# Feature-major products with hi and lo activations in one stream, two PSUM sums, and SBUF in hi/lo pairs

## The chip, the cores and the metric

One core of a Trainium2 chip runs the whole program. Its engines are TensorE (PE, with PEld for the load of a stationary operand), VectorE (DVE), ScalarE (ACT), GpSimd (POOL, not used here after the start) and SyncE (SP, which issues most transfers). The metric is the device time of one execution in microseconds (us); lower is better.

## The reference

Two layers of a hybrid block over 256 tokens of width 1024, all in float32. Everything that matters here is a product of activations with a weight matrix:

```python
for l in range(DEPTH):                       # DEPTH = 2
    h = rms_norm(x, norm_mix_pre[l])
    zq, zk, zv, zx, zy, zxq, zg = in_projection(h, w_in[l])
    ...                                      # rotary on q and k
    y_attn = diff_attention(q, k, v, lam, diff_subln[l], lam_init)
    xc = causal_conv(zx, conv_w[l], conv_b[l])
    y_lru = rg_lru(xc, ...) * jax.nn.gelu(zy)
    y_mem = memory_attention(zxq, mem, norm_mem[l], w_kv_mem[l])
    gates = jax.nn.sigmoid(zg.reshape(B, S, N_BRANCH, D_MODEL) + b_gate[l])
    merged = (gates[:, :, 0] * (y_attn @ w_proj_attn[l])
              + gates[:, :, 1] * (y_lru @ w_proj_lru[l])
              + gates[:, :, 2] * (y_mem @ w_proj_mem[l]))
    x = x + rms_norm(merged @ w_out[l], norm_mix_post[l])
    h = rms_norm(x, norm_mlp_pre[l])
    a = jax.nn.relu(h @ w_mlp_up[l])
    x = x + rms_norm((a * a) @ w_mlp_down[l], norm_mlp_post[l])
```

## The kernel before

Each float32 operand of a large product is held as two parts in the rounded type float32r: hi is the value rounded for TensorE, lo is the rest of it. A product is three matmuls: hi·hi, lo·hi and hi·lo.

**Weight stream.** The weights come in chunks of 1 MB, 128 partitions by 2048 values, in the order of their use (`layer_plan`, `full_plan`; 186 chunks: 184 of the two kinds below and twice the gate weights `rg`). SP loads a chunk into one of three `raw` buffers. Each half of a chunk is split by one ACT cast (`wh`, L155) and one DVE subtraction (`wl`, L157), into one of five `hl` buffers each; `weights` runs the splits up to `AHEAD` = 5 halves ahead of their use.

**Feature-major products** (`mm_feat`, L213 to L223) have the weights stationary and the activations moving: a chunk gives two tiles of 128 features by 256 tokens. For each of the two halves and each of eight contraction tiles k there are three matmuls of 256 columns, L219 (wh with the hi part), L220 (wh with the lo part) and L221 (wl with the hi part), all into the same 256 columns of one PSUM tile `acc` (one bank of 512 values, four buffers). They are used for the memory keys (`mk`), the queries of the cross attention (`xq`), the inputs `x` and `y` of the recurrent branch, `q` and `k`, the gates `g0` to `g2`, the branch projections `pm`, `pl`, `pa`, and the `up` product of the MLP: 64 chunks in a layer, 128 in all. **Token-major products** (`mm_tok`, L225 to L252: `mv`, `v`, `wo`, `dn`, 28 chunks in a layer) have the activations stationary and the weights moving, 512 columns in each matmul, three matmuls again (L233, L234, L235).

**Who reads a feature-major sum.** The reader of each chunk takes it straight from PSUM: DVE first in `rotary` (L607 to L610, for q and k), in the `up` product (L877), in the projections (L830, L832) and the memory keys; ACT first for `xq` (a split), `conv` (L530), `gelu2` (L538) and the gates (`tanh`, L822).

**Side work.** The cross attention (`xattn`), the recurrent gates and scan (`lru`), the attention (`attn`) and the transposes (`transposed`) are generators that advance by one step after half chunks (`tick`) or are run to their end (`flush`). Their TensorE work stands between half chunks of the weight stream, in the PSUM pools `at` and `sc`; their DVE and ACT work shares those engines with the splits and with the readers of the sums. A scheduler sets the final order of each engine's queue from the priorities and the dependences; each engine then runs its queue in order.

**SBUF.** Activations take whole buffers of 128 x 2048 values (`a8`, twelve of them), the hi and the lo part each one.

Of the kernel before, what the change touches and what calls it, by code (L numbers as in the profile page):

```python
# [17 lines left out]
D = 1024  # L18
# [7 lines left out]
# vectors of the feature-major parameter tile, 8 columns each  # L26
# [6 lines left out]
def layer_plan(l):  # L33
    """Weight chunks of a layer in the order in which they are used: (name, index)."""
# [34 lines left out]
def trunk(ctx, tc, x_in, xt_in, mem_in, memt_in, w_in, par_in, lamv_in, post_in, rope_in, out):  # L69
# [13 lines left out]
    def a8(name, dt=F32):  # L83
        return p_a8.tile([128, 2048], dt, tag="a8", name=name)
# [13 lines left out]
    def acc():  # L98
        return ps_acc.tile([128, 512], F32, tag="acc", name="acc")
# [4 lines left out]
    # ---------------- constants and parameters  # L104
# [26 lines left out]
    # ---------------- weight stream  # L131
# [14 lines left out]
    def issue_split(u):  # L146
# [6 lines left out]
        lo = p_hl.tile([128, 1024], F32R, tag="wl", name="wl")  # L153
        for sl in ((slice(0, 512), slice(512, 1024)) if u == 0 else (slice(0, 1024),)):
            act.copy(h[:, sl], r[:, sl])  # L155
            with tc.issue_after(state["hold"]) if state["hold"] is not None else nullcontext():
                dve.tensor_tensor(lo[:, sl], r[:, sl], h[:, sl].bitcast(F32), op=ALU.subtract)  # L157
        hl_t[u] = (h, lo)
# [91 lines left out]

    def rsqrt(ss, n, mul):
        """1 / sqrt(ss * mul + eps) of n columns, by Newton steps."""  # L252
# [12 lines left out]
    def rsqrt2(v):  # L265
        """1 / sqrt(v) of each column, the table's value refined by a Newton step."""
# [9 lines left out]
    def transposed(src, gain, h, lo):  # L276
        """Rows of src transposed and times gain, as hi and lo parts."""
        for j in range(4):
# [5 lines left out]
            for i in range(2):  # L284
                f = 2 * j + i
                split_to(f8(h)[:, f, :], f8(lo)[:, f, :], ps[:, i * 256:(i + 1) * 256], gain[:, f:f + 1])
            yield

    def rms(src, junk):
        """1 / rms of the rows of src."""  # L290
# [7 lines left out]
    def normed(src):  # L298
        """RMS-normalised rows of src."""
# [6 lines left out]
    def row_of(r, row):  # L306
        """row[p, token] = r[token] for every p."""
# [48 lines left out]
    # ---------------- parameters worked out once  # L356
# [42 lines left out]
    # ---------------- memory keys and values  # L399
# [4 lines left out]
    def mem_rms():  # L404
        t = a8("memr").rearrange("p (t n) -> p t n", t=2)
        load_rows(t, mem_in)
        j = a8("mj").rearrange("p (t n) -> p t n", t=2)
        dve.tensor_copy(mr, rms(t, j))

    def gained(src, gain, name):  # L410
        """Feature-major rows times gain, as hi and lo parts."""
        h, lo = a8(name + "h", F32R), a8(name + "l", F32R)
        for f in range(8):
            split_to(f8(h)[:, f, :], f8(lo)[:, f, :], f8(src)[:, f, :], gain[:, f:f + 1])
        return h, lo
# [4 lines left out]
    def mem_keys(l, hook=None):  # L420
        kh, kl = a8("kh", F32R), a8("kl", F32R)
        pend = []
        for j in range(4):
            ps = acc()
            mm_feat(ps, (l, "mk", j), mhat[l])
# [3 lines left out]
            if j > 0:  # L429
                for i, p in pend:  # L430
# [3 lines left out]
                    split_to(kh[:, sl], kl[:, sl], k)  # L434
                pend = []
            tick()
        kmem[l] = (kh, kl)

    def mem_values(l, hook=None):
        vh, vl = (a8(n, F32R) for n in ("vh", "vl"))  # L440
        mh, ml = mhat.pop(l)
        for n in range(2):
            pss = [acc(), acc()]
            for c in range(2):
                mm_tok(pss, (l, "mv", 2 * n + c), lambda k: (f8(mh)[:, 4 * c + k, :], f8(ml)[:, 4 * c + k, :]), c == 0, c == 1)
# [4 lines left out]
            for t in range(2):  # L450
                sl = slice(t * 1024 + n * 512, t * 1024 + (n + 1) * 512)
                split_to(vh[:, sl], vl[:, sl], pss[t], mr[:, t:t + 1])
            tick()
        vmem[l] = (vh, vl)

    # ---------------- cross attention (side work)
    def xattn(l, xq, ym):
        qh, ql = (f8(t) for t in xq)
        kh, kl = (f8(t) for t in kmem.pop(l))
# [533 lines left out]
```

## Time and profile before

| | us |
|---|---|
| median of 3 runs (1153.3 to 1154.36) | 1153.54 |
| span of the profiled execution | 1151.0 |
| median less span | 2.5 |
| PE busy, share of the span | 98% |
| DVE busy | 69% |
| ACT busy | 56% |

The span runs from the first to the last instruction of the profiled execution; the times are those of whole executions, so about 2.5 us lie around the span. The profiled execution's own time is not listed apart from the three; its span is the figure that stage by stage sums are made against, and 2.5 us are added to compare with the median. Shares of busy time of PE count a matmul from its start to its modelled end, so that a row's mean is longer than the beat at which matmuls follow each other; the beat is read from the starts in the timeline.

### The profile page before, as it was taken

To read this page: it belongs to the slowest core of one execution; us is meant where nothing else is said; L and a number is where in the kernel's file an instruction comes from. 1 tells how busy PE (TensorE), PEld (TensorE's weight loads), DVE (VectorE), ACT (ScalarE), POOL (GpSimd) and SP (SyncE) were. 2 spreads that over 40 slices of the span, in tenths; PEclk is the share of its full clock that TensorE was granted. 3 is DMA by queue.
4 is the path that set the end of the run, shared out by engine and by line. 5 is a ranking of instruction groups with operands and counts; after the bars stand their busy time and mean duration, and the time that the engine had idled before them with its cause. 6 is when DMAs were issued, how large, how long until landed. Compare 5 with 4: busy or idle time off the path is not lost.

```text
span 1151.0 us, 19712 instructions
## 1 busy us (share of the span) xinstructions
PE 1133.0 (98%) x8144; PEld 1067.1 (93%) x8144; DVE 792.0 (69%) x1219; ACT 644.7 (56%) x984; POOL 0.7 (0%) x6
## 2 busy tenths in 40 slices
PE   7999999999999999999999999999999998999997
PEld 6899999899999899998888999989999997999886
DVE  6868779788756676664557677887876566766453
ACT  6745585665455656554446556846654455655342
POOL 0000000000000000000000000000000000000000
PEclk9999999999999999999999999999999999999999
DMA  9665346643455545555555633664435553555550
GB/s 326 244 220 184 110 167 203 243 156 128 168 213 202 190 169 176 184 171 217 179 210 180 218 111 140 206 226 161 147 147 184 202 183 126 177 184 202 207 185 37
DMA packets 34793, 209.53 MB, mean 182 GB/s; under 512 B 3856, under 2 KB 8080, under 8 KB 10768
## 3 DMA queue, kind: packets, MB, share of 16 engines
q1 hardware_dynamic: 34128, 206.18, 50.2%
q10 hardware_dynamic: 576, 2.10, 0.5%
q8 instruction: 64, 1.05, 0.4%
q14 instruction: 25, 0.20, 0.0%
HBM read 203.02 MB, written 1.05 MB: 177 GB/s over the span
## 4 chain that ended last, share of the span: by engine, by line
PE 97%; DVE 2%; DMA 0%; ACT 0%; issue 0%; SPq 0%; DVEq 0%
PE acc L221 21%; PE acc L219 21%; PE acc L220 21%; PE acc L235 9%; PE acc L234 9%; PE acc L233 9%; PE at L555 1%; PE sc L638 1%; PE at L508 1%; PE at L473 1%; PE at L673 1%; DMA raw<-in_w 0%; PE at L283 0%; DVE wl L157 0%; PE at L493 0%; PE at L688 0%
## 5 line engine op out<-in xcount | busy, mean ns | idle before, releaser
L157 DVE TENSOR_TENSOR wl<-raw,wh 128x1024 fp32r<-128x1024 f32 (+1 forms) x369 | 449.2, 1221 | 258.7 <-ACT wh L155 257.6
L155 ACT CAST wh<-raw 128x1024 fp32r<-128x1024 f32 (+1 forms) x369 | 384.6, 1046 | 384.7 <-PE acc L220 251.4
L219 PE MATMUL acc<-hh,wh 128*128 128x256 f32 x1536 | 438.1, 286 | 0.2 <-ACT hh L209 0.2
L220 PE MATMUL acc<-hl,wh 128*128 128x256 f32 x1536 | 435.0, 283 | 0.5 <-DVE hl L210 0.5
L221 PE MATMUL acc<-hh,wl 128*128 128x256 f32 x1536 | 435.2, 284 | 0.0
L219 PEld LDWEIGHTS acc<-hh,wh 128*128 128x128 f32 x1536 | 294.6, 192 | 1.6 <-ACT wh L155 0.7
L220 PEld LDWEIGHTS acc<-hl,wh 128*128 128x128 f32 x1536 | 295.0, 192 | 1.0 <-DVE hl L210 0.7
L221 PEld LDWEIGHTS acc<-hh,wl 128*128 128x128 f32 x1536 | 294.7, 192 | 0.7 <-issue 0.7
L233 PE MATMUL acc<-wh,sqh 128*128 128x512 f32 x256 | 99.6, 389 | 0.0
L234 PE MATMUL acc<-wl,sqh 128*128 128x512 f32 x256 | 99.6, 389 | 0.0
L235 PE MATMUL acc<-wh,sql 128*128 128x512 f32 x256 | 99.6, 389 | 0.0
L233 PEld LDWEIGHTS acc<-wh,sqh 128*128 128x128 f32 x256 | 48.1, 188 | 10.0
L234 PEld LDWEIGHTS acc<-wl,sqh 128*128 128x128 f32 x256 | 48.1, 188 | 10.0
L235 PEld LDWEIGHTS acc<-wh,sql 128*128 128x128 f32 x256 | 48.1, 188 | 9.8
L219 PE MATMUL acc<-mhh,wh 128*128 128x256 f32 x128 | 38.0, 297 | 6.7 <-ACT wh L155 6.7
L221 PE MATMUL acc<-mhh,wl 128*128 128x256 f32 x128 | 37.5, 293 | 0.7 <-DVE wl L157 0.7
L220 PE MATMUL acc<-mhl,wh 128*128 128x256 f32 x128 | 37.6, 294 | 0.1
L219 PE MATMUL acc<-xqh,wh 128*128 128x256 f32 x128 | 36.8, 288 | 0.0
L219 PE MATMUL acc<-ylh,wh 128*128 128x256 f32 x128 | 36.7, 287 | 0.0
L648 ACT ACTIVATE ae<-sc,anm 128x128 f32<-128x128 f32 (+1 forms) x64 | 26.3, 416 | 18.4 <-DVE anm L644 15.4
L221 PE MATMUL acc<-xqh,wl 128*128 128x256 f32 x128 | 36.4, 285 | 0.0
L221 PE MATMUL acc<-ylh,wl 128*128 128x256 f32 x128 | 36.2, 283 | 0.0
(215 smaller groups left out, 1693.2 us busy)
## 6 DMA issues: line engine op xcount, KB each, us to landing
raw<-in_w SPq DMA_DIRECT2D x183, 1024.0 KB, 4.8
rgw<-in_w SPq DMA_DIRECT2D x2, 1024.0 KB, 6.9
qT<-rq SPq DMA_DIRECT2D x16, 128.0 KB, 2.3
kT<-rk SPq DMA_DIRECT2D x16, 128.0 KB, 2.3
gb<-in_post ACTq DMA_DIRECT2D x4, 512.0 KB, 5.0
mem<-in_memt SPq DMA_DIRECT2D x4, 256.0 KB, 5.7
memr<-in_mem SPq DMA_DIRECT2D x2, 512.0 KB, 7.3
xt<-in_x SPq DMA_DIRECT2D x2, 512.0 KB, 9.5
```

The costliest lines, as they stand in the source:

```text
L155: act.copy(h[:, sl], r[:, sl])
L157: dve.tensor_tensor(lo[:, sl], r[:, sl], h[:, sl].bitcast(F32), op=ALU.subtract)
L219: pe.matmul(o, wh[:, k, :], ah[:, k, :], start=(k == 0), stop=False)
L220: pe.matmul(o, wh[:, k, :], al[:, k, :], start=False, stop=False)
L221: state["mm"] = pe.matmul(o, wl[:, k, :], ah[:, k, :], start=False, stop=(k == 7))
L233: pe.matmul(pss[t], ah[:, sl], wh[:, k, :], start=(first and half == 0 and k == 0), stop=False)
L234: pe.matmul(pss[t], ah[:, sl], wl[:, k, :], start=False, stop=False)
L235: m = pe.matmul(pss[t], al[:, sl], wh[:, k, :], start=False, stop=(last and half == 1 and k == 1))
L473: pe.matmul(o, a[:, k, ts], b[:, k, :], start=(n == 0), stop=(n == 5))
L508: pe.matmul(o, a[:, m, fs], b[:, ms], start=(n == 0), stop=(n == 5))
L555: pe.matmul(ps[:, i * 256:(i + 1) * 256], wv[:, c, f, :], xv[:, f, :], start=True, stop=True)
L648: act.activation(out=e[:, c * nk:(c + 1) * nk], in_=sv[:, c, :], func=AF.Exp, bias=nm[:, c:c + 1], accum_out=ss[:, c:c + 1])
```

## The change

In a feature-major product the hi and the lo part of the activations now stand in one buffer (`pair`, 128 x 4096 values, hi in the first half and lo in the second), and pass wh in one matmul of 512 columns made of two runs of 256: hi·wh lands in columns 0 to 255 of a PSUM bank and lo·wh in columns 256 to 511. wl with the hi part follows as a matmul of 256 columns into columns 0 to 255. Each half of a chunk now fills one bank, so `acc` has two banks and there are two such buffers in place of four of one bank. After the chunk, ACT copies the right halves of both banks to SBUF (`z`, a `tmp` buffer) and DVE adds the left halves; `mm_feat` gives `z` to the reader, which no longer reads PSUM. SBUF is dealt out in six pairs in place of twelve singles; what needs only a single buffer takes a pair (`a8`), or two such needs share one (`duo`). `mm_tok` keeps its matmuls. Comments and docstrings went as well.

```diff
-    p_a8 = ctx.enter_context(tc.tile_pool(name="a8", bufs=12))
+    p_pair = ctx.enter_context(tc.tile_pool(name="pair", bufs=6))
...
-    ps_acc = ctx.enter_context(tc.tile_pool(name="psacc", bufs=4, space=bass.MemoryType.PSUM))
+    ps_acc = ctx.enter_context(tc.tile_pool(name="psacc", bufs=2, space=bass.MemoryType.PSUM))
...
-    def a8(name, dt=F32):
-        return p_a8.tile([128, 2048], dt, tag="a8", name=name)
+    def pair(name):
+
+        return p_pair.tile([128, 4096], F32R, tag="pair", name=name)
...
+    def hl(t):
+
+        return t.rearrange("p (s k n) -> p s k n", s=2, k=8)
+
+    def duo(name):
+
+        t = p_pair.tile([128, 4096], F32, tag="pair", name=name)
+        return t[:, 0:2048], t[:, 2048:4096]
+
+    def a8(name):
+        return duo(name)[0]
...
     def acc():
-        return ps_acc.tile([128, 512], F32, tag="acc", name="acc")
+
+        return ps_acc.tile([128, 2, 512], F32, tag="acc", name="acc")
+
+    def acc_tok():
+        a = acc()
+        return [a[:, t, :] for t in range(2)]
...
-    def mm_feat(ps, key, a):
-        """Two feature tiles of 256 tokens: weights stationary."""
-        ah, al = (f8(t) for t in a)
+    def mm_feat(key, a):
+
+
+
+
+        ps = acc()
+        av = hl(a)
         for j in range(2):
             wh, wl = (f8(t) for t in weights(*key, j))
-            o = ps[:, j * 256:(j + 1) * 256]
+            o = ps[:, j, :]
             for k in range(8):
-                pe.matmul(o, wh[:, k, :], ah[:, k, :], start=(k == 0), stop=False)
-                pe.matmul(o, wh[:, k, :], al[:, k, :], start=False, stop=False)
-                state["mm"] = pe.matmul(o, wl[:, k, :], ah[:, k, :], start=False, stop=(k == 7))
+                pe.matmul(o.rearrange("p (s n) -> p s n", s=2), wh[:, k, :], av[:, :, k, :], start=(k == 0), stop=False)
+                state["mm"] = pe.matmul(o[:, 0:256], wl[:, k, :], av[:, 0, k, :], start=False, stop=(k == 7))
             if j == 0:
                 tick()
+        z = tmp("z")
+        act.copy(two(z), ps[:, :, 256:512])
+        dve.tensor_tensor(two(z), two(z), ps[:, :, 0:256], op=ALU.add)
+        return z
...
-                ps = acc()
-                mm_feat(ps, (l, nm, j), hx)
+                ps = mm_feat((l, nm, j), hx)
                 rotary(scale, j, ps, r)
...
-            pss = [acc(), acc()]
+            pss = acc_tok()
```

**What stands where.** DVE, in the q and k products of the first layer, before: the subtraction for the weights (`wl`), the rotary steps that read `acc`, and a step of the recurrent branch (`xc<-xc,lE`).

```order
L157 TENSOR_TENSOR wl<-raw,wh 128x1024
L607 SCALAR_TENSOR_TENSOR rp_1956<-acc,rope 128x512
L608 SCALAR_TENSOR_TENSOR rp_1957<-acc,rope 128x256
L609 SCALAR_TENSOR_TENSOR rp_1957<-acc,rope 128x256
L157 TENSOR_TENSOR wl<-raw,wh 128x1024
L610 TENSOR_TENSOR rq<-rp_1956,rp_1957 128x2x256
L583 SCALAR_TENSOR_TENSOR xc<-xc,lE 128x512
```

DVE, at the same place, now (`xcg` is the former `xc`, `rqk` the former `rq`):

```order
L253 TENSOR_TENSOR z<-z,acc 128x512
L181 TENSOR_TENSOR wl<-raw,wh 128x1024
L641 SCALAR_TENSOR_TENSOR rp_1682<-z,rope 128x512
L642 SCALAR_TENSOR_TENSOR rp_1683<-z,rope 128x256
L643 SCALAR_TENSOR_TENSOR rp_1683<-z,rope 128x256
L181 TENSOR_TENSOR wl<-raw,wh 128x1024
L644 TENSOR_TENSOR rqk<-rp_1682,rp_1683 128x2x256
L617 SCALAR_TENSOR_TENSOR xcg<-xcg,lE 128x512
```

Each chunk has one more DVE instruction, L253, which stands ahead of a `wl` and waits for the ACT copy L252; the rest kept its order.

ACT, in the y product of the first layer, before: the first reader of the sum (`gq<-acc`) is on ACT, followed by the tanh of the recurrent gate, the second half of the GeLU, and a cast of weights.

```order
L155 CAST wh<-raw 128x1024
L538 ACTIVATE gq<-acc 128x512
L561 ACTIVATE lT<-at,hbi 128x256 x2
L540 ACTIVATE gq<-gq 128x512
L155 CAST wh<-raw 128x1024
```

ACT, at the same place, now:

```order
L179 CAST wh<-raw 128x1024
L252 COPY z<-acc 128x512
L595 ACTIVATE lru<-at,hbi 128x256 x2
L572 ACTIVATE gq<-z 128x512
L179 CAST wh<-raw 128x1024
L574 ACTIVATE gq<-gq 128x512
```

ACT copies first, and its own reading of the sum (L572) comes after DVE's addition; a cast of weights now stands between the two halves of the GeLU.

PE, at the end of the second layer's `wo` product and the start of its `up` product, before: transposes of the new x (`at<-ident,xt`), then the first matmuls of three half chunks as the parts of h come in.

```order
L235 MATMUL acc<-wh,mgl 128x512
L283 MATMUL at<-ident,xt 128x128 x8
L219 MATMUL acc<-hh,wh 128x256 x3
L220 MATMUL acc<-hl,wh 128x256
L221 MATMUL acc<-hh,wl 128x256
```

PE, at the same place, now:

```order
L266 MATMUL acc<-wh,mp 128x512
L318 MATMUL at<-ident,xt 128x128 x8
L247 MATMUL acc<-hx,wh 128x512
L248 MATMUL acc<-hx,wl 128x256
L247 MATMUL acc<-hx,wh 128x512
L248 MATMUL acc<-hx,wl 128x256
L318 MATMUL at<-ident,xt 128x128 x4
```

Three matmuls with the hi part alone stood ahead of the first one with the lo part; now the first one reads both parts.

## Rows read from the trace of the kernel before

**Rows 1.** The page: busy time by engine, and TensorE's granted clock in 40 slices

```profile
PE 1133.0 (98%) x8144; PEld 1067.1 (93%) x8144; DVE 792.0 (69%) x1219; ACT 644.7 (56%) x984; POOL 0.7 (0%) x6
...
PEclk9999999999999999999999999999999999999999
```

**Rows 2.** The page: the chain that ended last, by engine and by line

```profile
PE 97%; DVE 2%; DMA 0%; ACT 0%; issue 0%; SPq 0%; DVEq 0%
PE acc L221 21%; PE acc L219 21%; PE acc L220 21%; PE acc L235 9%; PE acc L234 9%; PE acc L233 9%; PE at L555 1%; PE sc L638 1%; PE at L508 1%; PE at L473 1%; PE at L673 1%; DMA raw<-in_w 0%; PE at L283 0%; DVE wl L157 0%; PE at L493 0%; PE at L688 0%
```

**Rows 3.** Groups by line: shapes, count | busy us, mean ns | idle before, releaser

```profile
L157 DVE TENSOR_TENSOR wl<-raw,wh 128x1024 fp32r<-128x1024 f32 x367 | 447.8, 1224 | 258.1 <-ACT wh L155 257.1
L220 PE MATMUL acc<-hl,wh 128*128 128x256 f32 x1536 | 435.0, 283 | 0.5 <-DVE hl L210 0.5
L155 ACT CAST wh<-raw 128x1024 fp32r<-128x1024 f32 x367 | 383.4, 1048 | 384.4 <-PE acc L220 251.4 <-PE acc L235 108.3 <-issue 16.9
L220 PEld LDWEIGHTS acc<-hl,wh 128*128 128x128 f32 x1536 | 295.0, 192 | 1.0 <-DVE hl L210 0.7
L331 ACT ACTIVATE junk<-acc 128x512 f32<-128x512 f32 x16 | 9.5, 596 | 19.3 <-PE acc L235 19.3
L335 DVE TENSOR_TENSOR yg<-acc,gb 128x512 f32<-128x512 f32 x12 | 8.2, 686 | 6.1 <-DMA gb<-in_post 3.2 <-ACT junk L331 3.0
```

**Rows 4.** Timeline of PE in the up product: start us, us, instruction

```profile
440.08 0.28 PE L220 MATMUL acc<-hl,wh 128*128 128x256 f32 x1
...
442.96 0.28 PE L220 MATMUL acc<-hl,wh 128*128 128x256 f32 x1
```

**Rows 5.** Timeline of PE in the down product

```profile
548.27 0.39 PE L233 MATMUL acc<-wh,sqh 128*128 128x512 f32 x1
...
553.03 0.39 PE L233 MATMUL acc<-wh,sqh 128*128 128x512 f32 x1
```

**Rows 6.** Stretches: us, busy of PE, PEld, DVE, ACT, POOL, clock, DMA share, GB/s

```profile
20.00:46.00 26.00, 26.00 (x178) 24.10 (x176) 18.78 (x37) 19.51 (x28) 0.00 (x0) 1.00 0.91 356
...
147.00:193.00 46.00, 46.00 (x385) 46.00 (x384) 39.78 (x57) 35.78 (x49) 0.00 (x0) 1.00 0.59 199
...
216.00:262.00 46.00, 46.00 (x383) 42.61 (x382) 38.06 (x79) 31.77 (x76) 0.00 (x0) 1.00 0.44 161
262.00:315.00 53.00, 53.00 (x450) 52.53 (x449) 41.61 (x101) 27.29 (x49) 0.00 (x0) 1.00 0.43 151
...
510.00:597.00 87.00, 87.00 (x386) 72.08 (x385) 43.50 (x45) 38.43 (x45) 0.00 (x0) 1.00 0.55 200
...
957.00:965.00 8.00, 4.50 (x23) 3.68 (x22) 7.64 (x17) 4.99 (x13) 0.00 (x0) 0.81 0.15 20
```

**Rows 7.** Timeline of DVE in the first layer's q and k products

```profile
164.14 0.69 DVE L583 SCALAR_TENSOR_TENSOR xc<-xc,lE 128x512 f32<-128x512 f32 x1
164.75 0.68 DVE L607 SCALAR_TENSOR_TENSOR rp<-acc,rope 128x512 f32<-128x512 f32 x1
...
190.00 4.42 DVE L592 TENSOR_TENSOR_SCAN xc<-lA,lT 128x2048 f32<-128x2048 f32 x1
194.34 2.34 DVE L157 TENSOR_TENSOR wl<-raw,wh 128x1024 fp32r<-128x1024 f32 x2
```

**Rows 8.** Timeline in the second layer's first gate chunk: its last matmul, its reader

```profile
784.91 0.28 PE L221 MATMUL acc<-hh,wl 128*128 128x256 f32 x1
...
789.90 0.84 ACT L822 ACTIVATE th<-acc,hbg 128x256 f32<-128x256 f32 x2
790.07 0.99 PE L638 MATMUL sc<-kT,qT 64*128 64x128 f32 x8
```

**Rows 9.** Timeline at the end of the first layer's cross attention

```profile
120.01 0.68 DVE L207 TENSOR_TENSOR xpl<-at,xph 128x512 fp32r<-128x512 f32 x1
...
121.15 0.28 PE L508 MATMUL at<-xpl,vh 128*128 128x256 f32 x1
```

**Rows 10.** Timeline of PE at the start of the second layer's up product

```profile
959.77 0.88 PE L283 MATMUL at<-ident,xt 128*128 128x128 f32 x6 [2.65 <-DVE xt L352]
960.88 0.62 PE L219 MATMUL acc<-hh,wh 128*128 128x256 f32 x3 [0.24 <-ACT hh L209]
961.96 0.58 PE L220 MATMUL acc<-hl,wh 128*128 128x256 f32 x1 [0.46 <-DVE hl L210]
```

More of the change, by code (lines that the diff above doesn't have):

```diff
@@ L152, in issue_split @@
         h = p_hl.tile([128, 1024], F32R, tag="wh", name="wh")
-        lo = p_hl.tile([128, 1024], F32R, tag="wl", name="wl")
+        l = p_hl.tile([128, 1024], F32R, tag="wl", name="wl")
         for sl in ((slice(0, 512), slice(512, 1024)) if u == 0 else (slice(0, 1024),)):
@@ L274, in rsqrt2, with transposed @@
         return y
-    def transposed(src, gain, h, lo):
+    def transposed(src, gain, a):
         for j in range(4):
@@ L285, in transposed @@
                 f = 2 * j + i
-                split_to(f8(h)[:, f, :], f8(lo)[:, f, :], ps[:, i * 256:(i + 1) * 256], gain[:, f:f + 1])
+                split_to(hl(a)[:, 0, f, :], hl(a)[:, 1, f, :], ps[:, i * 256:(i + 1) * 256], gain[:, f:f + 1])
             yield
@@ L404, in mem_rms @@
     def mem_rms():
-        t = a8("memr").rearrange("p (t n) -> p t n", t=2)
+        t, j = (a.rearrange("p (t n) -> p t n", t=2) for a in duo("memr"))
         load_rows(t, mem_in)
-        j = a8("mj").rearrange("p (t n) -> p t n", t=2)
         dve.tensor_copy(mr, rms(t, j))
     def gained(src, gain, name):
-        h, lo = a8(name + "h", F32R), a8(name + "l", F32R)
+        a = hl(pair(name))
         for f in range(8):
-            split_to(f8(h)[:, f, :], f8(lo)[:, f, :], f8(src)[:, f, :], gain[:, f:f + 1])
-        return h, lo
+            split_to(a[:, 0, f, :], a[:, 1, f, :], f8(src)[:, f, :], gain[:, f:f + 1])
+        return a.rearrange("p s k n -> p (s k n)")
     def mem_gained(l):
@@ L451, in mem_values @@
                 sl = slice(t * 1024 + n * 512, t * 1024 + (n + 1) * 512)
-                split_to(vh[:, sl], vl[:, sl], pss[t], mr[:, t:t + 1])
+                split_to(hi(va)[:, sl], lo(va)[:, sl], pss[t], mr[:, t:t + 1])
             tick()
-        vmem[l] = (vh, vl)
+        vmem[l] = va
     def xattn(l, xq, ym):
-        qh, ql = (f8(t) for t in xq)
-        kh, kl = (f8(t) for t in kmem.pop(l))
-        vh, vl = (t.rearrange("p (t n) -> p t n", t=2) for t in vmem.pop(l))
-        yh, yl = ym
+        q, k_ = hl(xq), hl(kmem.pop(l))
+        vm = vmem.pop(l)
+        vh, vl = (t.rearrange("p (t n) -> p t n", t=2) for t in (hi(vm), lo(vm)))
+        yh, yl = hi(ym), lo(ym)
         es, phs = {}, {}
@@ L471, in scores @@
                 for k in (2 * h, 2 * h + 1):
-                    for a, b in ((qh, kh), (qh, kl), (ql, kh)):
-                        pe.matmul(o, a[:, k, ts], b[:, k, :], start=(n == 0), stop=(n == 5))
+                    for a, b in ((0, 0), (0, 1), (1, 0)):
+                        pe.matmul(o, q[:, a, k, ts], k_[:, b, k, :], start=(n == 0), stop=(n == 5))
                         n += 1
@@ L593, in lru @@
         yield
-        yh, yl = yl_
+        ylr = done["y"] = pair("ylr")
         for j in range(4):
@@ L621, in by_head, with attn @@
                                       in_=rv[32 * g:32 * g + 32, i, :, :])
-    def attn(l, qT, kT, va, ya):
+    def attn(l, qT, kT, va, done):
         qv, kv = f8(qT), f8(kT)
         vv = va.rearrange("p (t n) -> p t n", t=2)
-        yh, yl = (f8(t) for t in ya)
         pbs, pts, os = {}, {}, {}
@@ L688, in back @@
                 pe.transpose(pt[:, i * 128:(i + 1) * 128], o[:, i * 128:(i + 1) * 128], ident)
-            split_to(yh[:, 4 * g:4 * g + 4, b * 128:(b + 1) * 128], yl[:, 4 * g:4 * g + 4, b * 128:(b + 1) * 128],
+            if "y" not in done:
+                done["y"] = pair("ya")
+            y = hl(done["y"])[:, :, 4 * g:4 * g + 4, b * 128:(b + 1) * 128]
+            split_to(y[:, 0], y[:, 1],
                      pt.rearrange("p (h t) -> p h t", h=4), sgain[:, l:l + 1])
@@ L757, in trunk @@
             hat = normed(xt)
-            hx = (a8("hh", F32R), a8("hl", F32R))
-            job = side(transposed(hat, par[:, l, P_MIX, :], *hx))
+            hx = pair("hx")
+            job = side(transposed(hat, par[:, l, P_MIX, :], hx))
             job["n"] = -3
@@ L790, in trunk @@
         flush(j_x)
-        qT, kT, va = a8("qT"), a8("kT"), a8("va")
-        for nm, scale, dst in (("q", 0.125, qT), ("k", 1.0, kT)):
-            r = a8("r" + nm)
+        qT, kT = duo("qkT")
+        va, mg = duo("vmg")
+        rq, rk = duo("rqk")
+        for nm, scale, dst, r in (("q", 0.125, qT, rq), ("k", 1.0, kT, rk)):
             for j in range(4):
-                ps = acc()
-                mm_feat(ps, (l, nm, j), hx)
+                ps = mm_feat((l, nm, j), hx)
                 rotary(scale, j, ps, r)
@@ L806, in trunk @@
                 act.copy(va[:, t * 1024 + n * 512:t * 1024 + (n + 1) * 512], pss[t])
-        ya = (a8("yah", F32R), a8("yal", F32R))
+        ya = {}
         j_a = side(attn(l, qT, kT, va, ya))
-        mg = a8("mg")
-        for b, pj, yb in ((2, "pm", ym), (1, "pl", ylr), (0, "pa", ya)):
+        for b, pj, yb in ((2, "pm", {"y": ym}), (1, "pl", ylr), (0, "pa", ya)):
             if b == 1:
@@ L852, in trunk @@
         state["ahead"] = AHEAD
-        hx = (a8("hh", F32R), a8("hl", F32R))
+        hx = pair("hx")
         hrow = p_sm.tile([128, 256], F32, tag="hrow", name="hrow", bufs=1)
-        job = side(transposed(xt, par[:, l, P_MLP, :], *hx))
+        job = side(transposed(xt, par[:, l, P_MLP, :], hx))
         if l + 1 == DEPTH:
@@ L863, in trunk @@
             flush(job)
-        sqs = [(a8("sqh", F32R), a8("sql", F32R)) for _ in range(4)]
+        sqs = [pair("sq") for _ in range(4)]
         pend = []
         for j in range(16):
-            ps = acc()
-            mm_feat(ps, (l, "up", j), hx)
+            ps = mm_feat((l, "up", j), hx)
             pend.append((j, ps))
```

87 lines of the change are left out of this document (43 added, 44 removed).

## The prediction

> **What bounds the kernel now.** [...] A busy PE could still be a waiting PE, so the chain of waits comes next: 97% of it is PE, and the three lines of the feature-major products hold 21% each, 63% together [rows 2]. The groups by line say the same from the other side: the 1536 matmuls of L220 with h follow 0.5 us of idle time in all, while ACT's cast waits 251.4 us for PE, because the splits are ahead and wait for a free buffer [rows 3]. So the time is the sum of the beats at which matmuls follow each other, and what DVE and ACT do costs nothing as long as it stays ahead.
>
> The beat comes from starts, not from row lengths. In the up product two starts 24 matmuls apart lie 2.88 us apart: **120 ns for 256 columns** [rows 4]. In the down product two starts 21 matmuls apart lie 4.76 us apart: **226.7 ns for 512 columns** [rows 5]. [...] A load of weights takes 192 ns as a row [rows 3], more than the beat of 120 ns, so the loads lie beside the matmuls.
>
> **The change, part by part.**
>
> *Fewer, longer matmuls.* Columns stay the same (768 for each contraction tile), but there are two matmuls in place of three: 226.7 + 120 = 346.7 ns for 3 x 120 = 360 ns. There are 128 chunks x 2 halves x 8 tiles = 2048 such groups, so PE's work shrinks by 2048 x 13.3 ns = **27.3 us**, 0.21 us in each chunk of 5.76 us, which becomes 5.55 us. No row shows a moving operand made of two runs; the nearest is the 512 columns in one run of [rows 5]. From below the bound is that figure; from above, that the second run costs a start of its own, 240 ns, and nothing is gained. [...]
>
> [...]
>
> *The way out of PSUM.* Each chunk adds an ACT copy of 512 values from PSUM and a DVE addition with one input in PSUM. The nearest rows are L331 with 596 ns and L335 with 686 ns [rows 3]; DVE instructions of this size follow each other at 0.61 us [rows 7]. That is 128 x 0.6 = 77 us more of ACT and 128 x 0.61 = 78 us more of DVE. They lie beside PE, and the cover is the lead of the splits: a split starts when the half five places ahead has been used up and is needed four halves later, 4 x 2.88 us, less 1.05 us for the cast and 1.22 us for the subtraction [rows 3] is about 9.2 us. The new waits are three. DVE's addition waits for ACT's copy, and behind it stands a wl subtraction. ACT's first readers (gates, conv, GeLU, xq) now wait for DVE's addition, and behind them stand casts of weights. PE's first matmul of a chunk waits for the addition of the chunk two before, and behind it stands all of PE. Reading SBUF instead of PSUM I cost at nothing: L583 without and L607 with a PSUM input take 0.69 and 0.68 us [rows 7]. I look at each place where the cover is thin.
>
> 1. *q and k, both layers (147 to 193 us and its like).* DVE is busy 39.78 of 46 us, ACT 35.78 [rows 6]. Eight chunks add 4.9 us to DVE and 4.8 to ACT, and PE takes 8 x 0.21 = 1.7 us less: DVE 44.7 and ACT 40.6 of 44.3 us. DVE is full. At the end stands the scan of 4.42 us, with two subtractions (2.34 us) queued behind it [rows 7]. If DVE uses its 6.2 us of idle time well, it falls back by 0.4 us and PE feels nothing; if it can use none, by 6.6 us, and 9.2 - 4.4 - 2.3 = 2.5 us of lead leaves a stall of 4.1 us. I take 1 us in each layer, **2 us** in all, range 0 to 8.2.
>
> 2. *The attention (216 to 315 us and its like).* DVE 38.06 of 46 and 41.61 of 53 us [rows 6]; with seven and eight additions and less time some 42.3 of 44.5 and 46.5 of 51.3. Full in places. The longest way out: a gate chunk's last matmul ends at 785.19, and ACT reads the sum at 789.90, 4.7 us later [rows 8]. With copy and addition the buffer would be free 4.7 + 0.6 + 0.7 = 6.0 us after the end; PE comes back to it after one chunk of 5.55 us and side work like the 0.99 us of L638 [rows 8], 6.5 us. So two buffers just do. I take 0.5 us in each layer, **1 us**, range 0 to 6.
>
> 3. *The end of the cross attention.* DVE ends the lo part of the probabilities at 120.69, and PE reads it at 121.15 [rows 9]: 0.46 us to spare. A copy or an addition ahead of it in a queue adds 0.6 to 1.2 us. Two heads in each layer are that close: **1 us**, range 0 to 3.
>
> 4. *The start of the second layer's up product.* PE waits here anyway and the clock's mean is 0.81 [rows 6]. The first matmul ran at 960.88 with the hi part, the first with the lo part at 961.96 [rows 10]; a stream of both starts 1.1 us later, and two half chunks instead of three have work to offer. [...] **1.5 us**, range 0.5 to 3.
>
> 5. *The start.* From 20 to 46 us the DMA engines are 91% busy [rows 6], so the 4 x 0.21 = **0.9 us** of the first four chunks are not gained; range 0 to 1.7, by how many of the first eight chunks this holds for.
>
> *SBUF in pairs.* The same 96 KB in six pieces. In the order of the built program the first instructions on each of them stand within a chunk or so of where they stood, and the last of the four buffers for the squares waits for the end of the up product in both versions. No row shows a wait for such a buffer; I cost it at nothing, and it is part of the ranges above.
>
> *The rest.* The token-major products keep their beat; that they run 87 us at 226.7 ns, with a 1 MB chunk every 24 x 226.7 ns = 5.44 us and DMA at 55% [rows 6], shows that weights can come faster than the new feature-major chunks of 5.55 us ask.
>
> **Sum.** 27.3 - 2 - 1 - 1 - 1.5 - 0.9 = 20.9 us off the span of 1151.0, which becomes about 1130. The median stands 2.5 us above the span: 1153.5 - 20.9 = **1133 us**, a gain of 1.8%.
>
> **The rivals.**
>
> *A: DVE and ACT become the bound in the loaded stages.* The same places at their upper ends: 8.2 + 6 + 3 + 3 + 1.7 = 21.9 us lost of 27.3, so 1148 us; 1139 to 1149 with only some of them. For it: DVE at 44.7 of 44.3 us. Against it: the lead of 9 us, and that DVE's waits now are mostly for casts that wait for PE [rows 3].
>
> *B: the fixed part does not go away* (it ends on the other side). The place is the first matmul of each of the 2048 groups. If the second run of its moving operand costs a start, the beat is 240 ns, the 27.3 us are not there, and the losses 1 to 4 remain: 1153.5 + 5.5 = 1159 us. It decides from the point where the 512-column matmul beats at more than 226.7 + 20.9 / 2.048 = 236.9 ns; between, the time is within 0.2% of before. For it: no row has two runs. [...]
>
> *C: PE waits at every chunk for one of only two buffers.* From 0.21 us for each of 128 chunks the gain is gone; 0.25 us would give 1158 us. Against it: way out 0.6 + 0.7 us, plus what stands ahead, in a chunk of 5.55 us; only the attention's 4.7 us come near.
>
> *D: loads are not hidden, and each of the 2048 that go comes off the path.* At 192 ns [rows 3] that would be 393 us, 760 us in all. Against it: a beat shorter than the load. [...]
>
> **How the numbers follow.** Forecast (1126 to 1139): 0.74. A: 0.14. B: 0.08, of which 0.02 within 0.2%. C: 0.03, about 0.01 of it within 0.2%. D: 0.01. A measurement of this kernel can tell about 0.2% (2.3 us) from no change. Faster by more than that: 0.74 + 0.14 + 0.01 = 0.89; within: 0.03; slower: 0.08. The range must leave out no more than 0.2: from 1125, where hardly any loss comes (27.3 us less 0 to 1), to 1146, most of A.
>
> **What would show it right or wrong.** In the up product the starts of successive 512-column matmuls should lie 0.347 us apart; 0.36 means B. Between 147 and 193 us and 216 and 315 us DVE should be near full; PE idle time put down to DVE's wl means A, to DVE's z (the addition) means C. In the up stage PE should have no idle time at all. The stage of the down product should take 87 us as before. Wrong would be the whole sum if matmuls with two runs have another beat than 226.7 ns, since all else is small.

## The result and the profile after

The changed kernel takes 1163.16 us (median of 4 runs, 1162.32 to 1163.42), the kernel before on the same chip 1153.42 us: a ratio of 1.0082, 95% interval 1.0068 to 1.0097. It is **slower by 0.8%**. Forecast were 1133 us and a range of 1125 to 1146 us; time and sign are wrong.

The page of the changed kernel, beside [rows 1] and [rows 2]:

```profile
PE 1122.5 (97%) x6096; PEld 956.6 (82%) x6096; DVE 863.4 (74%) x1347; ACT 705.2 (61%) x1112; POOL 0.7 (0%) x6
...
PEclk9999999989999999999999999999999998999998
...
PE 27%; DVE 3%; ACT 1%; issue 0%; DVEq 0%; ACTq 0%
```

PE's busy time fell by 10.5 us, but its time without work grew by 20.6 (1151.0 - 1133.0 = 18.0 before, 1161.1 - 1122.5 = 38.6 now), and the granted clock is below its upper level in a part of three slices. The chain's shares add up to only 31%, since it could not be followed back further; it says less here than the waits. The view of waits names what PE waited for (us in all, times, longest):

```profile
PE acc L247 <- ACT wh L179: 8.0, 4, 6.5
PE at L318 <- DVE xt L388: 5.3, 2, 3.9
PE sc L670 <- ACT ae L680: 4.0, 2, 2.0
PE acc L247 <- DVE z L253: 3.1, 6, 0.7
PE acc L247 <- ACT vmg L835: 2.9, 2, 1.4
PE acc L248 <- DVE wl L181: 2.8, 4, 0.8
```

The 6.5 us of the first line are the wait for the first weights at the start. In the kernel before, the same view has 6.7 us for these weights, 2.9 us for the transposes of x (`at<-ident,xt`), and nothing else above 0.7 us. The groups by line have the sizes that [rows 3] gave for the way out: 580 ns for ACT's copy, 681 ns for DVE's addition (taken were 0.6 and 0.61 us):

```profile
L253 DVE TENSOR_TENSOR z<-z,acc 128x512 f32<-128x512 f32 x128 | 87.1, 681 | 8.7 <-ACT z L252 8.7
L252 ACT COPY z<-acc 128x512 f32<-128x512 f32 x128 | 74.3, 580 | 9.5 <-PE acc L248 9.4
```

The beat, by starts in the timeline of PE (beside [rows 4]), first in the first layer's q, then in its up product:

```profile
160.10 0.39 PE L247 MATMUL acc<-hx,wh 128*128 128x512 f32 x1
...
163.57 0.39 PE L247 MATMUL acc<-hx,wh 128*128 128x512 f32 x1
...
439.89 0.40 PE L247 MATMUL acc<-hx,wh 128*128 128x512 f32 x1
...
442.01 0.40 PE L247 MATMUL acc<-hx,wh 128*128 128x512 f32 x1
```

In q ten pairs of a 512- and a 256-column matmul take 3.47 us, 347 ns each, as forecast; in up six pairs take 2.12 us, 353 ns each, half the gain over 360 ns. PE has **two rhythms** in the new stream, and in the whole kernel 102 half chunks keep the faster one and 152 the slower (2 were too disturbed to tell). Each half chunk has eight pairs, and each pair gains what its half chunk's mean lies under 360 ns: summed up, the stream gave 19.0 us, not 27.3.

A table by stage shows where the 29.1 us went that turn this into +10.1 us of span. A stage runs from its first matmul to that of the next; "lost" is the change of its time plus what the stream gave in it.

| stages | change, us | stream gave | lost | lost, forecast | lost with one SBUF pair moved (below) |
|---|---|---|---|---|---|
| start, mk, mv, xq, first layer | +0.6 | 1.0 | 1.6 | 0.9 | 2.3 |
| x, y, q, k, both layers | -5.1 | 5.6 | 0.5 | 3 | 0.5 |
| v, both | +3.7 | 0 | **3.7** | 0 | 0.5 |
| g2 and pm, both | +10.9 | 2.4 | **13.3** | 1, with g1 | 2.5 |
| g1 and pl, both | +1.3 | 2.4 | 3.7 | | 3.6 |
| g0 and pa, both | -1.7 | 1.7 | 0.0 | 0 | 0.0 |
| wo to xq between the layers | -2.2 | 2.7 | 0.5 | 0 | 0.5 |
| wo, up, dn of the second layer | -0.1 | 3.3 | 3.2 | 1.5 | 3.4 |
| after the last matmul | +2.7 | 0 | **2.7** | 0 | 2.7 |
| sum | +10.1 | 19.0 | 29.1 | 6.4 | 16.1 |

Most of the loss lies at one place of each layer, from the end of v through the first gates. The timeline of ACT there (first layer):

```profile
204.16 0.62 ACT L230 CAST ylr<-xcg 128x512 fp32r<-128x512 f32 x1 [4.11 <-DVE xcg L631]
204.69 2.00 ACT L179 CAST wh<-raw 128x1024 fp32r<-128x1024 f32 x2
207.64 0.62 ACT L230 CAST ylr<-xcg 128x512 fp32r<-128x512 f32 x1 [0.95 <-DVE xcg L631]
211.11 1.22 ACT L230 CAST ylr<-xcg 128x512 fp32r<-128x512 f32 x2 [2.85 <-DVE xcg L631]
213.10 2.06 ACT L835 COPY vmg<-acc 128x512 f32<-128x512 f32 x4 [0.76 <-DVE ylr L231]
218.97 1.28 ACT L680 ACT_TABLE_LOAD   x1 [3.82 <-DVE anm L676]
```

ACT's four copies of v stand behind all four casts of `ylr`, the end of the recurrent branch, and start when DVE's last `ylr` subtraction is done; the first two of those sums were complete half-way through v, near 201.5 us. In the kernel before, the copies of v (`va<-acc`) stood among these casts, and the first two ran half-way through v:

```profile
203.79 0.62 ACT L206 CAST ylh<-xc 128x512 fp32r<-128x512 f32 x1 [0.76 <-DVE xc L597]
204.31 0.58 ACT L806 COPY va<-acc 128x512 f32<-128x512 f32 x1
...
213.49 0.59 ACT L806 COPY va<-acc 128x512 f32<-128x512 f32 x1 [4.59 <-PE acc L235]
```

In the changed kernel PE then waits 1.43 us for a tile, ACT waits 3.82 us for the scores with casts of weights queued behind, and PE waits for these casts and their subtractions. Behind 242.52 it waits again, 1.99 us for the scores' tile:

```profile
214.22 0.50 PE L247 MATMUL acc<-hx,wh 128*128 128x512 f32 x1 [1.43 <-ACT vmg L835]
...
221.71 0.49 PE L247 MATMUL acc<-xq,wh 128*128 128x512 f32 x1 [0.53 <-ACT wh L179]
...
222.97 0.39 PE L248 MATMUL acc<-xq,wl 128*128 128x256 f32 x1 [0.77 <-DVE wl L181]
...
244.78 0.93 PE L670 MATMUL sc<-qkT 64*128 64x128 f32 x8 [1.99 <-ACT ae L680]
```

The second layer shows the same waits of PE at the same places (1.43, 0.53, 0.76 and 1.99 us).

### The profile page after: what moved, and what is told of

It is laid out like the page before. It is cut to its first block, busy times and chain, and to the rows that moved or that the text cites. A ratio compares the mean times of both kernels' runs of the same rounds, so it can differ in the third digit from the quotient of the medians.

```text
span 1161.1 us, 15842 instructions
## 1 busy us (share of the span) xinstructions
PE 1122.5 (97%) x6096; PEld 956.6 (82%) x6096; DVE 863.4 (74%) x1347; ACT 705.2 (61%) x1112; POOL 0.7 (0%) x6
## 5 line engine op out<-in xcount | busy, mean ns | idle before, releaser
L247 PE MATMUL acc<-hx,wh 128*128 128x512 f32 x1536 | 550.3, 401 | 6.5 <-ACT vmg L835 2.9
L248 PE MATMUL acc<-hx,wl 128*128 128x256 f32 x1536 | 432.9, 282 | 0.0
L247 PEld LDWEIGHTS acc<-hx,wh 128*128 128x128 f32 x1536 | 290.1, 189 | 77.4 <-ACT vmg L835 3.7
L248 PEld LDWEIGHTS acc<-hx,wl 128*128 128x128 f32 x1536 | 292.0, 190 | 2.5 <-issue 2.0
L266 PE MATMUL acc<-wh,sq 128*128 128x512 f32 x256 | 99.6, 389 | 0.0
L265 PE MATMUL acc<-wl,sq 128*128 128x512 f32 x256 | 99.6, 389 | 0.0
L264 PE MATMUL acc<-wh,sq 128*128 128x512 f32 x256 | 99.6, 389 | 0.0
L253 DVE TENSOR_TENSOR z<-z,acc 128x512 f32<-128x512 f32 x128 | 87.1, 681 | 8.7 <-ACT z L252 8.7
L252 ACT COPY z<-acc 128x512 f32<-128x512 f32 x128 | 74.3, 580 | 9.5 <-PE acc L248 9.4
L265 PEld LDWEIGHTS acc<-wl,sq 128*128 128x128 f32 x256 | 48.1, 188 | 10.0
L264 PEld LDWEIGHTS acc<-wh,sq 128*128 128x128 f32 x256 | 48.1, 188 | 10.0
L266 PEld LDWEIGHTS acc<-wh,sq 128*128 128x128 f32 x256 | 48.1, 188 | 9.9
```

The lines of the kernel that those rows point to most:

```text
L247: pe.matmul(o.rearrange("p (s n) -> p s n", s=2), wh[:, k, :], av[:, :, k, :], start=(k == 0), stop=False)
L248: state["mm"] = pe.matmul(o[:, 0:256], wl[:, k, :], av[:, 0, k, :], start=False, stop=(k == 7))
L252: act.copy(two(z), ps[:, :, 256:512])
L253: dve.tensor_tensor(two(z), two(z), ps[:, :, 0:256], op=ALU.add)
L264: pe.matmul(pss[t], ah[:, sl], wh[:, k, :], start=(first and half == 0 and k == 0), stop=False)
L265: pe.matmul(pss[t], ah[:, sl], wl[:, k, :], start=False, stop=False)
```

## The experiments

Two theories to begin with. **W**: the way out (128 copies and 128 additions) eats the gain. **T**: the coarse two-bank tile does. Four single steps lead from one version to the other; the first three are kernels of their own, the fourth is the changed kernel. Each ratio below is to the kernel before, measured beside that run on the same chip.

**Only the SBUF pairs.** Old products, one-bank tiles, readers in PSUM (the edit is against the changed kernel):

```diff
...
-                pe.matmul(o.rearrange("p (s n) -> p s n", s=2), wh[:, k, :], av[:, :, k, :], start=(k == 0), stop=False)
+                pe.matmul(o[:, 0:256], wh[:, k, :], av[:, 0, k, :], start=(k == 0), stop=False)
+                pe.matmul(o[:, 0:256], wh[:, k, :], av[:, 1, k, :], start=False, stop=False)
...
-        z = tmp("z")
-        act.copy(two(z), ps[:, :, 256:512])
-        dve.tensor_tensor(two(z), two(z), ps[:, :, 0:256], op=ALU.add)
-        return z
+        return ps
...
```

> The first of four steps that lead from the kernel before to the changed one: only SBUF is laid out in hi/lo pairs; the three 256-column matmuls, the four one-bank sums and the readers in PSUM are those of before. Theory W (the way out, ACT copy and DVE addition, eats the gain) and theory T (the two-bank tile that two sums share eats it): both expect the time of before, 1153.4 us, within 3 us. Theory P (the pairs delay something, since a pair comes free only as a whole): 1158 us or more.

1154.74 us, ratio 1.0011 (1.0002 to 1.0021); no stage after the start differs by over 0.1 us. By themselves the pairs cost next to nothing. But the timeline of ACT shows a wait that was not there before, the same one as above, with no harm yet:

```profile
209.12 1.08 ACT L832 COPY vmg<-acc 128x512 f32<-128x512 f32 x2 [0.17 <-DVE ylr L230]
213.55 0.59 ACT L832 COPY vmg<-acc 128x512 f32<-128x512 f32 x1 [3.35 <-PE acc L263]
```

In the kernel before the first copy of v ran at 204.31 us, as shown above.

**Two two-bank tiles as well** (`bufs=2`, `[128, 2, 512]`, old products):

> The second step: pairs, and two tiles of two banks each in place of four of one; both token sums share one tile, a feature chunk takes one tile too, but its three matmuls are the old 256-column ones and the readers read PSUM directly. Theory W: only the token sums' end is later (3.3 us ahead of the second layer's up product, 2.7 us after the last matmul, 1 us elsewhere), so about 1160 us. Theory T: the two tiles also stall PE where readers are late (v, the first gates), so about 1175 us or more.

1177.47 us, 1.0210 (1.0195 to 1.0226). The size is T's, the place is not: v and the gates lose nothing. The loss is at the start (mk +11.4 us) and in up (+4.0 and +1.8), where two sums wait in PSUM for the row of scales and so hold both tiles, in the second layer's wo (+3.0), and after the last matmul (+2.7, from the start of the last matmul to DVE's last instruction; called the tail below).

**The 512-column stream as well, without the way out** (`return ps[:, :, 0:256]`):

> The third step: as the changed kernel, but without the ACT copy and the DVE addition: the readers read the left half of the sum in PSUM directly, so the product of the lo activations with the rounded weights is computed and then left out of the result. Against the second step it shows the 512-column stream alone. All theories: 27 us less than the second step (13.3 ns for each of 2048 groups). Theory W: about 1133 us, 30 us below the changed kernel. Theory T: 1148 us or more, close to the changed kernel's 1163 us.

1159.01 us, 1.0059 (1.0037 to 1.0080): 18.5 us less than the step before, near the 19.0 us that the beats gave in the changed kernel. No stage from x to pa loses over 0.3 us. W's 1133 us are refuted; yet the way out, which makes only 4 us of difference in the sum, moves the loss: with it the first layer's mk and both up products take 14.3 us less, since the sums that had waited in PSUM there leave it early, and v to pl of both layers 19.9 us more.

**The way out alone, on the kernel before:**

```diff
+        z = tmp("z")
+        act.copy(z, ps)
+        dve.tensor_tensor(z, z, ps, op=ALU.max)
+        return z
...
```

> The kernel before, its three matmuls and four one-bank sums, with the way out added alone: ACT copies each chunk's 512 values to SBUF, DVE takes the maximum of copy and sum (the same values) into SBUF, and the readers read that. Theory W: PE loses in the attention and lru stages what it lost there in the changed kernel, some 20 to 30 us, so 1173 to 1183 us. Theory T: 1153 to 1158 us.

1156.25 us, 1.0023 (1.0013 to 1.0033). So neither part costs much alone, and W is refuted here too. What costs is a combination, and T would make the two-bank tile a part of it.

**One-bank tiles, way out by halves:**

```diff
...
-            o = ps[:, j, :]
+            o = acc()
...
+            act.copy(zj, o[:, 256:512])
+            dve.tensor_tensor(zj, zj, o[:, 0:256], op=ALU.add)
...
```

> The changed kernel with four tiles of one bank in place of two of two: each half chunk has a tile of its own, its way out (ACT copy of 256, DVE addition of 256 values) follows that half at once, and the two token sums of v, mv, wo and dn have a tile each. Theory T (what the changed kernel loses is the coarse two-bank tile: both token sums, or both halves, come free together, while the readers' queues are full): v back from 23.6 to 21.8 us, the first gates and pm (66 and 63 us) to about 58.5, the wo of the second layer from 30.2 to 26.5, the tail from 6.8 to 4.1; with a stream gain of 18 us and the 3 us of the way out alone some 1138 to 1143 us. Theory Q (full DVE and ACT queues lose it whatever the tiles are; 128 more copies and additions make them fuller): 1160 us or more.

1149.56 us, 0.9963 (0.9949 to 0.9977): between the theories. g2 and pm are back at 59.9 and 60.0 us and the tail at 4.1, but v stays at 23.3 us, and the copies of v still stand behind the `ylr` casts. T does not explain those.

**Hi and lo rows side by side, one run of 512 columns:**

```diff
-        return t.rearrange("p (s k n) -> p s k n", s=2, k=8)
+        return t.rearrange("p (k s n) -> p s k n", s=2, k=8)
...
```

> The changed kernel with the hi and lo rows of each contraction tile next to each other in SBUF, so that the 512 columns of the stream are one run in place of two; all else is the same. In the changed kernel a pair of matmuls (512 and 256 columns) follows the last in 353 ns in most half chunks and in 347 ns in the others. Theory R (the second run costs 7 ns of start in each stream, in the stages where it shows): 347 ns everywhere, up to 9 us off, 1154 us or so. Theory S (two steady rhythms of PE that have nothing to do with the layout): both rhythms still there, 1163 us within 4.

1162.25 us, 1.0068 (1.0050 to 1.0086). The seven largest groups of PE's waits add up to 27.3 us here and in the changed kernel, and the spans are 1160.2 and 1161.1 us: of the estimated 8.1 us that the slower rhythm takes (152 half chunks of eight pairs by 6.7 ns) 0.9 us are gone. So the second run is not what costs 7 ns. Together with the one-bank tiles:

> Both at once: tiles of one bank with the way out by halves, and hi and lo in one run of 512 columns. Theories T and R: 1130 to 1136 us. T and S: as with the one-bank tiles alone, 1138 to 1143 us. Q: 1155 us or more.

1149.77 us, 0.9963 (0.9948 to 0.9978), as with the tiles alone.

**A new theory, V: the SBUF pair.** In the built program the pair of `va` and `mg` lies where the pair of `xc` and `g2` lay, so the first copy of v has to wait for the last reader of `xc`, DVE's last `ylr` subtraction. Before, `va` had a buffer of its own and took that of `lA`, free after the scan. The test gives `va` and `mg` the pair that the scan has read last:

```diff
...
-        av, tv = duo("lru")
...
-        j_l = side(lru(l, xc, rgw, g2, ylr), 2)
+        va, mg = duo("lru")
+        j_l = side(lru(l, xc, rgw, g2, ylr, va, mg), 2)
...
-        va, mg = duo("vmg")
```

> The changed kernel with one pair of SBUF buffers moved: the values of the attention (va) and the merged sum (mg) lie in the pair that the recurrence's scan has read last (lru), where in the changed kernel they lie in a pair that is free only when the whole recurrent branch has ended (xcg). Theory V (the pair sharing makes ACT's four copies of v wait for the end of the recurrent branch, which the added DVE additions put off; the casts queued behind are late too): v back from 23.6 to 21.8 us in both layers, and the first gates and pm a few us shorter: 1152 to 1160 us. Theory X (the copies are late for another reason, the pairs cost nothing): 1163 us within 2.

1149.75 us, 0.9955 (0.9939 to 0.9972): **13.4 us less than the changed kernel** (12.9 by the spans of the profiled executions), below the 1152 to 1160 us that V expected, and faster than the kernel before. ACT there:

```profile
202.33 1.08 ACT L834 COPY lru<-acc 128x512 f32<-128x512 f32 x2 [1.66 <-PE acc L266]
...
213.43 1.07 ACT L834 COPY lru<-acc 128x512 f32<-128x512 f32 x2 [7.11 <-PE acc L266]
214.39 2.19 ACT L230 CAST ylr<-xcg 128x512 fp32r<-128x512 f32 x4
216.47 2.00 ACT L179 CAST wh<-raw 128x1024 fp32r<-128x1024 f32 x2
```

The copies follow PE again, and two casts stand ahead of the softmax. v loses 0.5 us in place of 3.7, g2 and pm 2.5 in place of 13.3 (last column of the table). The waits of 0.53, 0.77 and 1.99 us are gone, and with the last of them a stretch at the lower of the two clock levels (a granted clock of 0.50 from 246 to 252 us in the changed kernel; the upper level is 1.00). The stretch from 245 to 250 us, of the changed kernel and of this one (length, busy PE, PEld, DVE, ACT, POOL, clock as a mean over both levels, DMA share, GB/s):

```profile
245.00:250.00 5.00, 4.38 (x19) 3.52 (x18) 3.53 (x12) 1.92 (x7) 0.00 (x0) 0.57 0.21 87
```

```profile
245.00:250.00 5.00, 5.00 (x33) 3.99 (x32) 4.88 (x11) 3.54 (x10) 0.00 (x0) 1.00 0.46 136
```

The edit moves more than `va`: in the built program `ylr` now takes the pair of `rqk`, and `ya` that of `xcg`. That the copies of v are what counts is read from the releasers: ACT waited for DVE's `ylr` in the changed kernel and waits for PE here.

**The same on the one-bank tiles:**

> One-bank tiles with the way out by halves, and va and mg in the scan's pair. Theory V: the 2 x 1.5 us that v still loses with the one-bank tiles come back, and the wait for a cast in the first pm: 1144 to 1147 us. Theory X: 1149.6 us within 2.

1144.91 us, 0.9918 (0.9903 to 0.9933), as V expected. Here moving the SBUF pair is worth only 4.7 us, and the one-bank tiles with the pair left in place had the same 1149.6 us as the two-bank tiles with the pair moved. So neither the pair nor the tile is the cause alone: it takes three parts together for the whole of the loss. What v, g2 and pm lose in both layers, counted as in the table, is 17.0 us in the changed kernel, 3.0 with the pair moved, 7.3 with one-bank tiles and the pair left, 1.3 with both, and 0.2 with the pair and the two-bank tiles but without the way out.

Left is g1 and pl, 54.5 and 54.4 us, against 51.2 before. DVE there, then PE:

```profile
281.50 0.69 DVE L711 TENSOR_TENSOR ao<-at,ny 128x512 f32<-128x512 f32 x1
282.11 1.22 DVE L180 TENSOR_TENSOR wl<-raw,wh 128x1024 fp32r<-128x1024 f32 x1
283.24 0.75 DVE L250 TENSOR_TENSOR z<-z,acc 128x256 f32<-128x256 f32 x2
```

```profile
283.71 0.73 PE L247 MATMUL acc<-hx,wh 128*128 128x512 f32 x1 [2.34 <-DVE z L250]
```

The addition stands behind the attention's norm and a subtraction; PE waits 2.34 us for its tile.

**Old products in g1 and pl, and in the second layer's first up chunk, on the kernel just shown; then in g2 and pm too:**

```diff
+        if key[1] in ("g1", "pl") or key == (DEPTH - 1, "up", 0):
...
+            return ps
...
```

> As the last, but in the gates and the product of the second branch (g1, pl) of both layers, and in the first chunk of the second layer's up product, the three old 256-column matmuls in one bank, read from PSUM directly with no way out. With the one-bank tiles these stages take 54.5 and 53.0 us against 51.2 before, because PE waits there for the DVE addition. Theory L (the way out costs only where ACT and DVE are full, so the stream pays elsewhere): 51.2 us in both, 1138 to 1142 us. If the way out delays other stages too: 1143 us or more.

1141.39 us, 0.9887 (0.9872 to 0.9901): **the fastest here beside the next, 1.1% under the kernel before.** g1 and pl take 51.8 us, 0.6 above the 51.2 of before.

> As the last, with the old matmuls and no way out in the first branch's gates and product too (g2, pm). These 32 chunks give up 3.4 to 6.8 us of stream gain. Theory L: g2 and pm take 58.9 us as before against 59.9 with the one-bank tiles, 1137 to 1141 us. If the stream pays even there once the copies of v are early: slower than the last run by 1 to 3 us.

1141.52 us, 0.9885 (0.9870 to 0.9900): no difference. In each layer g2 and pm take 58.9 us in place of 58.2, since the stream's gain is gone, but g1 and pl behind them take 51.2 in place of 51.8.

**Two tiles for the last token sums**, on the kernel with `va` moved:

```diff
+    def acc_last():
+        return [acc()[:, 0, :], sc()[:, 0:512]]
...
-            pss = acc_tok()
+            pss = acc_last() if n == 1 else acc_tok()
...
```

> The changed kernel with va and mg in the scan's pair, and with the two last token sums of wo and dn in two tiles in place of one: token tile 0 in its accumulator, token tile 1 in the score tile, which is idle there. Theory T for the end of the residual branches (ACT reads token tile 0 only when the last matmul of both sums has ended, because dependences go by tile): the wo of the second layer back from 30.2 to about 26.5 us, the tail after the last matmul from 6.8 to 4.1 us, together 6 us off the 1149.8 us of the run with va moved: 1143 to 1145 us. If the reading of token tile 1 is what ends last anyway: 1149 us, no change.

1146.89 us, 0.9939 (0.9921 to 0.9956), 2.9 us less (2.5 by the spans; the intervals of the two ratios overlap). In the changed kernel, at the end of the second layer's wo, ACT reads the first sum only after the last matmul of both (PE, then ACT):

```profile
963.37 0.39 PE L266 MATMUL acc<-wh,mp 128*128 128x512 f32 x1
967.68 0.69 PE L318 MATMUL at<-ident,xt 128*128 128x128 f32 x2 [3.92 <-DVE xt L388]
969.78 1.54 PE L318 MATMUL at<-ident,xt 128*128 128x128 f32 x6 [1.41 <-DVE xt L388]
```

```profile
963.79 0.60 ACT L367 ACTIVATE junk<-acc 128x512 f32<-128x512 f32 x1 [0.30 <-PE acc L266]
```

With two tiles it reads it at 948.66, 2.3 us ahead of PE's last matmul at 950.96:

```profile
950.96 0.39 PE L269 MATMUL sc<-wh,mp 128*128 128x512 f32 x1
951.64 0.44 PE L321 MATMUL at<-ident,xt 128*128 128x128 f32 x2 [0.30 <-DVE xt L391]
954.73 1.54 PE L321 MATMUL at<-ident,xt 128*128 128x128 f32 x6 [2.65 <-DVE xt L391]
```

```profile
948.66 0.60 ACT L370 ACTIVATE junk<-acc 128x512 f32<-128x512 f32 x1 [1.66 <-PE acc L269]
```

The tail is back to 4.1 us, and wo to 27.5. But of these 2.6 us in wo up gives back 2.1, so half of the expected 6 us did not come: PE waits another 1.32 us before 959.89 for a part of h, and its first matmuls of up still run at the lower clock level, 0.50 and 0.51 in the two stretches from 955 to 965 us.

## Why the prediction was wrong

The span was forecast to fall by 20.9 us and rose by 10.1, a miss of 31.0 us. Of these, 8.3 are the stream (19.0 in place of 27.3), 13.0 went when the SBUF pair was moved (29.1 - 16.1), and 9.7 are the other places (16.1 lost in place of 6.4). "All else is small" was as wrong as the sign.

*The stream.* Two matmuls did take less time than three, 347 or 353 ns in place of 360, but the size was off: 19.0 us, not 27.3. I bounded the pair of matmuls by 346.7 and 360 ns and took the lower end. That a stream of two runs beats like one run of 512 columns, at 226.7 ns, was an estimate that no row of before showed; both the lower end and a value halfway, 353 ns, occur, so that 13.3 and 6.7 ns were measured for each matmul saved. Rival B took what two beats of 256 columns have over one of 512 (2 x 120 - 226.7 = 13.3 ns) for a fixed part and asked whether the second run costs it again; that is refuted, since with one run the kernel takes 1162.25 us and all but 0.9 of the estimated 8.1 us stay.

*The step that failed: "SBUF in pairs. [...] I cost it at nothing."* It gave the wrong sign: with that one pair moved the change is faster than before by 0.45%. I looked for waits in the profile of before, where a buffer that is not yet shared can show none, and let "within a chunk or so" pass in the built program. `va`'s first copy had come to stand two chunks later, behind the end of another branch: it runs 22.5 us after the start of v, before 11.4. That new dependence has slack to spare on its own (the pairs alone: +0.1%), and so has the way out (+0.2%). Together, with two sums in one tile that comes free only as a whole, they do not. The additions put off the scan: in [rows 7] it starts 2.9 us ahead of the end of k's matmuls (192.87 us), with the way out alone 2.8 us behind it, in the changed kernel 4.4 us behind (at 190.61 us):

```profile
194.98 4.42 DVE L626 TENSOR_TENSOR_SCAN xcg<-lru 128x2048 f32<-128x2048 f32 x1
```

The copies of v wait for what follows the scan, casts queue behind the copies, and PE waits for the casts. In the first layer the clock falls behind these waits too (0.50 from 246 to 252 us): g2 and pm take 65.6 us there and 63.1 in the second layer, which has the same waits and keeps its clock (1.00 from 781.75 to 844.82 us), so the fall cost an estimated 2.6 us. I priced each part against the whole slack of before; the pair, the way out and the coarse tile spent the same slack.

*"The token-major products keep their beat."* They do, but not the way out of their sums. Two sums in one tile come free and become readable together, since dependences go by tile here (the reading of the first sum at 963.79 us, and at 948.66 with two tiles); that is the 2.7 us after the last matmul, and part of the 3.2 us around the second layer's up (forecast 1.5, range 0.5 to 3). What the clock would add to the 1.5 us was an estimate that no row of before showed. PE's waits of 3.92, 1.41 and 0.65 us there are followed by a longer stretch at the lower clock level (0.50 from 966 to 976 us) than in the kernel before (0.50 from 962 to 965 us); the stretches with the first matmuls of up, of the kernel before and of the changed one:

```profile
960.00:965.00 5.00, 4.15 (x21) 3.44 (x20) 5.00 (x9) 3.84 (x9) 0.00 (x0) 0.69 0.24 33
965.00:970.00 5.00, 5.00 (x43) 5.00 (x42) 2.99 (x11) 2.88 (x5) 0.00 (x0) 0.97 0.43 180
```

```profile
970.00:975.00 5.00, 4.35 (x16) 3.27 (x16) 4.84 (x8) 3.91 (x9) 0.00 (x0) 0.50 0.17 33
975.00:980.00 5.00, 5.00 (x28) 4.41 (x27) 3.23 (x11) 1.74 (x5) 0.00 (x0) 0.89 0.43 177
```

*Places that were priced.* q and k, where I had DVE full, lost 0.1 us (range 0 to 8.2). I let DVE fall back by 0.4 us there, at most by 6.6; it fell back by 7.2, as the scan shows, and moved that work on behind k, so that it was busy only 39.95 us in the stage:

```profile
146.05:190.61 44.56, 44.56 (x259) 38.98 (x257) 39.95 (x62) 39.13 (x57) 0.00 (x0) 1.00 0.59 191
```

The splits' lead covered it, and the bill came at v. The attention was the right place to be wary of, with 16.9 us in place of 1 (range 0 to 6): 10.8 went when the pair was moved, 6.1 stay. The start lost 1.6 us, inside its range, and the cross attention's end with x and y 0.4 us.

*The rivals.* A came nearest in place, but asked for full engines; the engines were not full, their order was wrong. C's waits for `z` are there, 3.1 us in all, not one for each chunk. D's 393 us are not there.

**Still open:** what sets PE on either rhythm, why the clock fell behind the waits of one layer only, and how the 16.1 us that are lost with the pair moved divide between the way out and the tiles beyond the places shown.

## What to carry to other kernels

A change of buffer shapes is a change of dependences: for each buffer ask whose address it takes, who reads that last, and what is queued behind the first writer, in the built program of the new kernel, not in the profile of the old one. Parts that are harmless one at a time can share one piece of slack, so price them in sequence, each against what the others have left. And apply a faster product by stages: here it pays in up, q, k and g0, and on balance does nothing from g2 to pl, where its way out stands in the queues behind the attention's work.

## What the runs showed of the hardware

The pair of a 512- and a 256-column matmul repeats at 347 or at 353 ns while the granted clock is 1.00. In the changed kernel a rhythm can hold through whole stages without a break (347 ns in all eight half chunks of the first layer's k, 353 ns in all 32 of its up), and its changes come where other work or a wait stands between: at each of some 40 changes from one half chunk to the next, a pair in one of the two or between them starts over 0.4 us after the pair before it. The first layer's up product ran at 353 ns in the changed kernel; with one-bank tiles and the SBUF pair moved (the run of 1144.91 us) 29 pairs of it take 10.06 us, 347 ns each, from 435.63 to 445.69 us. The rhythm alone can so make an estimated difference of up to 1.7 us in one up product (256 pairs by 6.7 ns).

In the changed kernel's first layer a wait of PE of 1.99 us, and one of 0.62 us right after it, were followed by a granted clock of 0.57 in the mean of 5 us, though PE was busy 4.38 us of them. While 0.50 was granted, six pairs took 3.84 us (starts at 247.11 and 250.95 us), 640 ns each. In its second layer the same two waits (1.99 us before 812.38, 0.63 us before 813.93) were not followed by that: the clock stays at its upper level (1.00) in as long a stretch with as much work.

```profile
812.50:817.50 5.00, 4.37 (x29) 3.58 (x30) 3.62 (x12) 2.61 (x8) 0.00 (x0) 1.00 0.22 92
```

So the same waits can cost the clock or leave it, and these runs do not show what decides.
